# A conv-mixer block on one core: one SBUF operand for VectorE in the projection stage, seven convolution tiles on TensorE, and a new order for loads and first products

## The chip, the cores and the metric

The kernel runs on one core of a Trainium2 chip. The metric is device time in microseconds, the median of several runs on the chip; lower is better. Engines are named as the profile does: PE is TensorE, DVE is VectorE, ACT is ScalarE, POOL is GpSimd, SP is SyncE, whose queue issues almost all transfers here.

## The reference: what is computed

One layer of a decoder block on 256 tokens of width 2048, in float32, with random weights:

```
mod = silu(c) @ mod_w + mod_b                 # 2048 -> 6 x 2048: sh1, sc1, g1, sh2, sc2, g2
h = rms_norm(x, norm1_g) * (1 + sc1) + sh1
u = h @ w_in + b_in                           # 2048 -> 4096
a, gt = split(u);  u = a * sigmoid(gt)
u = depthwise causal convolution of 31 taps over the tokens (u) + dw_b
u = silu(layer_norm(u, ln_g, ln_b))
x = x + (1 + g1) * (u @ w_out + b_out)
h = rms_norm(x, norm2_g) * (1 + sc2) + sh2
x = x + (1 + g2) * (square(relu(h @ mlp_w1)) @ mlp_w2)   # 2048 -> 8192 -> 2048
```

## The kernel before, in words

**Layout.** Channels lie on the 128 partitions, tokens along the free axis: a tile is 128 channels by T=256 tokens, and the width is KT=16 such tiles. Weights come from HBM in float32 in blocks of 1 MB (128 x 16 x 128) into five `raw` buffers. Each block is split into a rounded part `hi` (ACT, L174) and the rest `lo` (DVE or POOL, L175); activations are split in the same way into `hl` tiles (L180, L181). A product is then hi·hi and hi·lo in one 512 wide matmul (L188) and lo·hi in a 256 wide one (L189). There are six half-block buffers for `hi` and six for `lo`.

**Jobs.** `jobs` is 16 input-projection jobs ("in"), 8 output-projection jobs ("out"), then four quarters of 8 "up" and 8 "down" jobs of the MLP. A job makes 256 output channels from all 16 input tiles: 64 matmuls into a PSUM tile `mm`, two of which exist.

**First stage** (L390 to L473). The squares of x (L336) are summed over the channels by PE (L287), and DVE makes the inverse root r (L291 to L307). The first seven in-jobs (HELD = 7) are not run job by job but input tile by input tile: seven PSUM tiles are held open, and for each k `first_mm` (L422) adds the products of the k-th input tile to all of them, in seven steps of six matmuls (L430, L433, L434). Their weights come through three `first` buffers of 0.9 MB. The scale and shift that each k needs come either as columns by DVE (`mod_col`, L259; b = 0 and 3 of the four groups of four k's) or as rows by PE (`mod_chunk`, L197, matmuls at L206, four 1 MB loads per 512 values; b = 1 and 2). In the loop at L438, each row chunk of b = 1 and 2 is followed by two product steps of the group before (L441 to L445).

**In stage** (loop at L634, jobs 7 to 15). Each job's matmuls are followed by the evacuation (`evac`, L383: ACT copies the second half, DVE adds, L387), the gate (L607: sigmoid L609 on ACT, product L613 on DVE) which makes u of this tile, and then by what CONV_AT lists for it. A convolution tile is done in one of two ways. Ten tiles are done by DVE as a chain of taps `acc = u[:, j:j+T] * w[j] + acc` (`conv_steps` L510, `tap` L491): the accumulator is a pair in PSUM, used in turn; the first tap is made by ACT into an SBUF tile `pre` (L502) and enters the third tap as its third operand; in tiles from 4 on the second tap takes the SBUF tile `shift` (L496), which is a common offset (minus the mean of the first two tiles) that is subtracted from every tile and keeps the layer norm's sums small. Six tiles (PE_TILES) are done by PE (`pe_conv` L568): u is written to a DRAM scratch `flat` (L581) and read back as a shifted `wide` tile in four transfers (L584), both on SP's queue, POOL builds diagonal weights (L587), and 64 small matmuls (L598) form the convolution. The last of them, tile 15, copies on chip instead (L570 to L578). Statistics (squares on ACT, sums on PE, L543 to L566) are taken four tiles at a time.

**Layer norm** (L667 to L693). After job 15: mean and mean square (ACT L680, L681; DVE L682, L683), the inverse root on DVE (L298 to L301), then for each pair of tiles the subtraction on POOL (L688), the product on DVE (L689), SiLU on ACT (L692) and the split. x is loaded a second time from POOL's queue (L697) for the residual in the out jobs.

**What sets the order.** All weight and modulation loads stand in one list, `order` (L363 to L375), and are issued on SP's queue in that order as buffers come free (`top_up`, L142); each is bound to be issued after the one before (L153). Everything else is placed by a scheduler that simulates the engines and writes one fixed order per engine; blocks under `urgent()` have priority, and `issue_after` puts an instruction behind a given one. The late modulation chunks (LATE_IN, LATE_OUT) are spread over the jobs and run as rows on PE between them. POOL makes the `lo` halves of all in jobs.

Of the kernel before, what the change touches and what calls it, by code (L numbers as in the profile page):

```python
# [8 lines left out]
F32 = mybir.dt.float32  # L9
# [55 lines left out]
def conv_block(ctx: ExitStack, tc: tile.TileContext, x, vec, dwq, c_row, mod_r, mod_c, w_first, w_in, w_out, w1, w2, out):  # L65
# [18 lines left out]
    xs = []  # L84

    def load_x(pool, queue):
        xs[:] = [pool.tile([P, 4, T], F32, name=f"x{i}") for i in range(4)]
        for i in range(4):
            queue.dma_start(xs[i], x[:, 4 * i : 4 * i + 4, :])

    start_scope = tc.tile_pool(name="start", bufs=1)
    start_pool = start_scope.__enter__()
    load_x(start_pool, nc.sync)
# [7 lines left out]
    modb1 = const.tile([P, KT], F32, name="modb1")  # L101
    nc.vector.tensor_scalar(modb1, col("modb", SC1 * KT, KT), 1.0, None, op0=ALU.add)
# [14 lines left out]
    waiting = {"raw": 0, "first": 0, "cond": 0}  # L117
    room = {"raw": RAW + 1, "first": FIRST + 1, "cond": 1}
    todo = []

    def source(key):
# [13 lines left out]
        if kind == "down":  # L135
            return w2[2 * key[2] + key[3], key[1]]
        return c_row

    def home(key):
        return "first" if key[0] == "first" else "cond" if key == ("c", 0) else "raw"  # L140

    def top_up():  # L142
        while todo and waiting[home(todo[0])] < room[home(todo[0])]:
# [5 lines left out]
            elif tag == "first":  # L149
                raw[key] = start_pool.tile([P, 2 * HELD, P], F32, name="first", bufs=FIRST)  # L150
            else:
                raw[key] = start_pool.tile([P, KT, P], F32, name="cond")
# [83 lines left out]
    def mod_bias(at, n, src):  # L236
        cs = slice(at, at + n)
        nc.vector.tensor_tensor(modc[:, cs], src, col("modb", at, n), op=ALU.add)
        which, k = divmod(at, KT)
        if which in amps:  # L240
            g = col("n1g" if which == SC1 else "n2g", k, n)
            nc.vector.scalar_tensor_tensor(amps[which][:, k : k + n], modc[:, cs], 1.0, g, op0=ALU.add, op1=ALU.mult)
        elif which in (G1, G2):
            nc.vector.tensor_scalar(modc[:, cs], modc[:, cs], 1.0, None, op0=ALU.add)
# [14 lines left out]
    def mod_col(at):  # L259
# [5 lines left out]
        if which == SC1:  # L265
            nc.vector.scalar_tensor_tensor(
                amps[SC1][:, k : k + 1], acc, modb1[:, k : k + 1], col("n1g", k), op0=ALU.add, op1=ALU.mult
# [555 lines left out]
```

## Time and profile before

| what | us |
|---|---|
| three timed runs | 1180.56, 1180.91, 1184.28 |
| median | 1180.91 |
| profiled execution, device time | 1182.57 |
| its span | 1180.8 |
| first product of the first stage | 28.10 |
| start of job 7 (end of the first stage) | 150.69 |
| start of job 8 | 173.67 |
| end of job 15 | about 320.5 |
| first matmul of the out jobs | 358.89 |

The profile is of one execution, recorded by the hardware. A line of a group reads: line of the code, engine, operation, output and inputs by name, shape, number of instructions, then busy time in us and the mean of one in ns, and after the second bar the engine's idle time just before them and what ended it. In the order in time, the two first numbers are the start and the length of a run of like instructions, in us from the start of the span. In the table of stretches, each engine has its busy time and number of instructions; then come the granted clock of TensorE as a share of full speed, the busy share of the 16 transfer engines and their GB/s. TensorE is busy for 95% of the span, but a busy TensorE can be at half clock, and the records of matmuls overlap.

### The profile page before, as it was taken

What the parts mean: (1) busy time and instruction counts of PE and PEld (TensorE: products, weight loads), DVE (VectorE), ACT (ScalarE), POOL (GpSimd) and SP (SyncE); (2) the same over time, 40 slices, a digit from 0 to 9 for tenths busy, and PEclk for the clock granted to TensorE, in tenths of its full rate; (3) what the DMA queues carried; (4) which work ended last, traced back from release to release, by engine and by line L of the source; (5) the groups of instructions that cost most, each with busy time, mean ns of one, the idle gap of its engine ahead of it and who ended that gap; (6) DMA issues with size and microseconds to landing.
All of it is one profiled execution on the core that took longest, in us unless ns stands there. A gap on an engine that the chain in (4) does not pass through costs nothing.

```text
span 1180.8 us, 17239 instructions
## 1 busy us (share of the span) xinstructions
PE 1121.2 (95%) x6962; PEld 936.1 (79%) x6962; DVE 773.3 (65%) x1066; ACT 565.5 (48%) x738; POOL 174.7 (15%) x124
## 2 busy tenths in 40 slices
PE   3959999989968999999999999999999999999998
PEld 2738967656546888888888888888888888888887
DVE  4635889999435797789777555555555556555553
ACT  5234443323336666855444555444555444555441
POOL 0000186545534224300000000000000000000000
PEclk9979999989988999999999999999999999999999
DMA  9998987779977894689888555555555555555640
GB/s 384 419 385 348 408 294 307 282 261 336 300 293 283 304 346 170 253 302 342 290 296 314 178 186 205 180 184 204 183 183 200 189 181 200 189 182 197 209 134 27
DMA packets 46159, 299.04 MB, mean 253 GB/s; under 512 B 5120, under 2 KB 8704, under 8 KB 12800
## 3 DMA queue, kind: packets, MB, share of 16 engines
q1 hardware_dynamic: 45216, 295.17, 68.5%
q0 software_dynamic: 576, 2.10, 0.5%
q8 instruction: 54, 0.88, 0.3%
q10 hardware_dynamic: 288, 0.69, 0.2%
q14 instruction: 25, 0.20, 0.0%
HBM read 295.10 MB, written 2.83 MB: 252 GB/s over the span
## 4 chain that ended last, share of the span: by engine, by line
PE 81%; DVE 14%; DMA 2%; ACT 1%; issue 1%; POOL 0%; SPq 0%; ACTq 0%; POOLq 0%; DVEq 0%
PE mm L188 46%; PE mm L189 24%; DVE acc L498 8%; PE row L206 2%; PE mm L598 2%; DVE raw L264 1%; PE mm L430 1%; PE mm L433 1%; PE mm L434 1%; DMA first<-w_first 1%; PE small L287 1%; DVE acc L496 1%; DVE lo L419 1%; DMA raw<-mod_r 1%; DVE two L387 0%
## 5 line engine op out<-in xcount | busy, mean ns | idle before, releaser
L188 PE MATMUL mm<-hl,hi 128*128 128x512 f32 x1504 | 533.0, 398 | 12.7 <-DVE hl L181 10.3
L174 ACT ACTIVATE hi<-raw 128x1024 fp32r<-128x1024 f32 x324 | 340.5, 1058 | 386.4 <-PE mm L188 356.5
L175 DVE TENSOR_TENSOR lo<-raw,hi 128x1024 fp32r<-128x1024 f32 x272 | 334.0, 1230 | 241.7 <-ACT hi L174 241.0
L189 PE MATMUL mm<-hl,lo 128*128 128x256 f32 x1504 | 424.3, 282 | 0.8 <-POOL lo L175 0.8
L188 PE MATMUL mm<-u,hi 128*128 128x512 f32 x1088 | 377.7, 390 | 0.0
L188 PEld LDWEIGHTS mm<-hl,hi 128*128 128x128 f32 x1504 | 284.1, 189 | 95.1 <-issue 13.0
L189 PE MATMUL mm<-u,lo 128*128 128x256 f32 x1088 | 307.1, 282 | 0.0
L189 PEld LDWEIGHTS mm<-hl,lo 128*128 128x128 f32 x1504 | 286.7, 191 | 8.8 <-issue 6.7
L188 PEld LDWEIGHTS mm<-u,hi 128*128 128x128 f32 x1088 | 204.3, 188 | 43.0 <-DVE small L301 0.2
L189 PEld LDWEIGHTS mm<-u,lo 128*128 128x128 f32 x1088 | 205.6, 189 | 0.0
L175 POOL TENSOR_TENSOR lo<-raw,hi 128x1024 fp32r<-128x1024 f32 x52 | 125.1, 2431 | 74.0 <-ACT hi L174 73.9
L498 DVE SCALAR_TENSOR_TENSOR acc<-u,v,acc 128x256 f32<-128x256 f32 x270 | 107.7, 476 | 0.0
L206 PE MATMUL row<-raw,cz 128*32 128x512 f32 x448 | 63.1, 622 | 12.2 <-DMA raw<-mod_r 11.2
L387 DVE TENSOR_TENSOR two<-mm,two 128x512 f32<-128x512 f32 (+1 forms) x74 | 50.0, 676 | 29.3 <-ACT two L386 28.1
L264 DVE SCALAR_TENSOR_TENSOR raw<-raw 128x2048 f32<-128x2048 f32 x24 | 57.8, 2410 | 13.6 <-DMA raw<-mod_c 10.7
L419 DVE TENSOR_TENSOR lo<-first,hi 128x896 fp32r<-128x896 f32 x32 | 34.3, 1086 | 41.5 <-ACT hi L418 41.5
L386 ACT ACTIVATE two<-mm 128x512 f32<-128x512 f32 (+1 forms) x74 | 42.7, 577 | 38.1 <-PE mm L189 37.6
L418 ACT ACTIVATE hi<-first 128x896 fp32r<-128x896 f32 x32 | 29.6, 944 | 38.0 <-PE mm L433 16.2
L181 DVE TENSOR_TENSOR u<-two,u 128x512 fp32r<-128x512 f32 x40 | 31.2, 779 | 23.4 <-ACT u L180 23.4
L430 PE MATMUL mm<-hl,hi 128*128 128x256 f32 x128 | 37.5, 302 | 8.7 <-ACT hl L180 8.7
L264 DVE SCALAR_TENSOR_TENSOR raw<-raw,cond 128x2048 f32<-128x2048 f32 x16 | 36.4, 2283 | 10.4 <-ACT cond L280 10.4
L433 PE MATMUL mm<-hl,hi 128*128 128x256 f32 x128 | 37.9, 298 | 1.7 <-DVE hl L181 1.7
(140 smaller groups left out, 754.8 us busy)
## 6 DMA issues: line engine op xcount, KB each, us to landing
raw<-w SPq DMA_DIRECT2D x128, 1024.0 KB, 4.9
raw<-mod_r SPq DMA_DIRECT2D x56, 1024.0 KB, 8.8
raw<-mod_c SPq DMA_DIRECT2D x40, 1024.0 KB, 7.3
raw<-w_in SPq DMA_DIRECT2D x18, 1024.0 KB, 8.5
raw<-w_out SPq DMA_DIRECT2D x16, 1024.0 KB, 6.3
first<-w_first SPq DMA_DIRECT2D x16, 896.0 KB, 11.0
wide<-flat SPq DMA_DIRECT2D x20, 142.0 KB, 8.2
x<-x SPq DMA_DIRECT2D x4, 512.0 KB, 6.9
```

Of the source, the lines that this page charges most:

```text
L174: nc.scalar.activation(hi, w[:, ks, :], AF.Copy)
L175: engine.tensor_tensor(lo, w[:, ks, :], hi.bitcast(F32), op=ALU.subtract)
L188: nc.tensor.matmul(p[:, c, :], hi[:, k % HALF, :], m, start=(k == 0), stop=(k == KT - 1))
L189: nc.tensor.matmul(p[:, c, T : 2 * T], lo[:, k % HALF, :], m[:, 0:T], start=False, stop=(k == KT - 1), skip_group_check=True,)
L206: state["row_end"] = nc.tensor.matmul(row_ps[0][32 * k : 32 * k + 32, :], cz[:, 4 * kg + k, 3 - b : 35 - b], w[:, 4 * k : 4 * k + 4, :], s ...
L264: nc.vector.scalar_tensor_tensor(w, w, 1.0, cb, op0=ALU.mult, op1=ALU.mult, accum_out=acc)
L386: nc.scalar.activation(t1, p[:, cs, T : 2 * T], AF.Copy)
L387: nc.vector.tensor_tensor(t2, p[:, cs, 0:T], t1, op=ALU.add)
L419: nc.vector.tensor_tensor(lo, w[:, js, :], hi.bitcast(F32), op=ALU.subtract)
L430: nc.tensor.matmul(p, hi[:, j, :], m[:, 0:T], start=(k == 0 and c == 0), stop=False, skip_group_check=True)
L433: nc.tensor.matmul(p, hi[:, j, :], m[:, T : 2 * T], start=False, stop=False, skip_group_check=True)
L498: nc.vector.scalar_tensor_tensor(out, s, w, acc, op0=ALU.mult, op1=ALU.add)
```

## The change

- **VectorE's operands.** `shift` no longer enters the taps of tiles below 12 (LATER): they are made without it and POOL adds it to four tiles at once (`shift(cvs[...], 4)`) ahead of their statistics. The first tap moves from ACT to DVE, with the bias, straight into the PSUM accumulator; the tile `pre` is gone. The evacuation of in jobs writes in place into PSUM, so that the gate reads PSUM. In the roots of the norms the mean square, its products and (in the layer norm) the factor lie in PSUM, and the square of the first guess is made by ACT. The additions of 1 to the modulation are folded into its bias at the start.
- **Tiles.** PE_TILES gets 9 and 12 and gives up 13: seven convolutions on PE, nine on DVE. Statistics of the first tiles move from after jobs 9, 11, 13 to after jobs 10, 13 and 15.
- **Scratch.** The `flat` transfer of PE tiles below 12 is issued after the last load issued so far at that point of the program.
- **First stage.** The squares of x go through two of the three `first` buffers. For b = 2, eight product steps go ahead of the row chunks, and one or two follow each (LEAD); row chunks are placed behind the last step's matmul.
- **x again.** The four x tiles are entries of the load list, right after the weights of out job 0, so they are issued on SP's queue ahead of the layer norm's end instead of on POOL's behind it. The convolution results move to a pool of their own.

In the order that the scheduler writes for the changed kernel, six row chunks (one more of them stands inside job 7) come ahead of the convolutions of tiles 0 and 1, and both ahead of job 8, where before the two convolutions stood among the first four chunks; three chunks and convolution 9 stand ahead of job 12, and convolution 10 ahead of job 13.

```diff
-PE_TILES = (0, 1, 10, 13, 14, 15)
-CONV_AT = {7: (0, 1, 2, 3), 8: (4,), 9: (5, 6), 10: (7,), 11: (8, 9), 12: (11,), 13: (10, 12), 14: (13,), 15: (14,)}
+PE_TILES = (0, 1, 9, 10, 12, 14, 15)
+CONV_AT = {7: (0, 1, 2, 3), 8: (4,), 9: (5, 6), 10: (7,), 11: (8, 9), 12: (11, 10), 13: (13,), 14: (12,), 15: (14,)}
-UNSHIFTED = (2, 3)
-STAT_AT = {9: 0, 11: 1, 13: 2}
+LATER = 12
+STAT_AT = {10: 0, 13: 1}
+LEAD = {1: 0, 2: 8}
...
-    modb1 = const.tile([P, KT], F32, name="modb1")
-    nc.vector.tensor_scalar(modb1, col("modb", SC1 * KT, KT), 1.0, None, op0=ALU.add)
+    for w in (SC1, G1, SC2, G2):
+        nc.vector.tensor_scalar(col("modb", w * KT, KT), col("modb", w * KT, KT), 1.0, None, op0=ALU.add)
...
     def mod_bias(at, n, src):
         cs = slice(at, at + n)
-        nc.vector.tensor_tensor(modc[:, cs], src, col("modb", at, n), op=ALU.add)
         which, k = divmod(at, KT)
         if which in amps:
             g = col("n1g" if which == SC1 else "n2g", k, n)
-            nc.vector.scalar_tensor_tensor(amps[which][:, k : k + n], modc[:, cs], 1.0, g, op0=ALU.add, op1=ALU.mult)
-        elif which in (G1, G2):
-            nc.vector.tensor_scalar(modc[:, cs], modc[:, cs], 1.0, None, op0=ALU.add)
+            nc.vector.tensor_tensor(src, src, col("modb", at, n), op=ALU.add)
+            nc.vector.tensor_tensor(amps[which][:, k : k + n], src, g, op=ALU.mult)
+        else:
+            nc.vector.tensor_tensor(modc[:, cs], src, col("modb", at, n), op=ALU.add)
...
-    def inverse_root(ms, then=None, where=None):
-        r = tmp.tile([P, T], F32, name="r", bufs=1) if where is None else where
-        q = tmp.tile([P, T], F32, name="q", bufs=1)
-        guess = tmp.tile([P, T], F32, name="guess", bufs=1)
+    def inverse_root(ms, r, then=None):
+        w = two()
+        guess, q = w[:, 0, :], w[:, 1, :]
         nc.scalar.activation(guess, ms, AF.Abs_reciprocal_sqrt)
+        nc.scalar.activation(q, guess, AF.Square)
...
-        nc.vector.tensor_tensor(q, guess, guess, op=ALU.mult)
-        nc.vector.tensor_tensor(q, q, ms, op=ALU.mult)
-        nc.vector.tensor_scalar(q, q, -0.5, 1.5, op0=ALU.mult, op1=ALU.add)
-        nc.vector.tensor_tensor(r, guess, q, op=ALU.mult)
+        nc.vector.tensor_tensor(ms, ms, q, op=ALU.mult)
+        nc.vector.tensor_scalar(ms, ms, -0.5, 1.5, op0=ALU.mult, op1=ALU.add)
+        nc.vector.tensor_tensor(r, ms, guess, op=ALU.mult)
...
-    def evac(p, cs=slice(0, 2)):
+    def evac(p, cs=slice(0, 2), out=None):
         t1 = two()[:, cs, :]
-        t2 = two()[:, cs, :]
+        t2 = two()[:, cs, :] if out is None else out
...
+    sq = [start_pool.tile([P, 2 * HELD, P], F32, name="first", bufs=FIRST) for _ in range(2)]
...
-        s = squares(xs[i])
+        s = squares(xs[i], sq[i % 2])
...
-            for key in first[b]:
-                mods([key])
+            for _ in range(LEAD[b]):
+                next(steps, None)
+            for at, key in enumerate(first[b]):
+                with tc.issue_after(state["step_end"].ins):
+                    mods([key])
                 with tc.issue_after(state["row_end"].ins):
-                    for _ in range(2):
+                    for _ in range(1 + at % 2 if LEAD[b] else 2):
                         next(steps, None)
...
+        if job == ("out", 0):
+            order += [("x", i) for i in range(4)]
...
-        if acc is None and (j > 1 or ct in UNSHIFTED):
+        if j == 0:
+            nc.vector.tensor_scalar(out, s, w, col("dwb", ct), op0=ALU.mult, op1=ALU.add)
+        elif acc is None and ct < LATER:
             nc.vector.tensor_scalar(out, s, w, None, op0=ALU.mult)
...
-    def first_tap(out, ct):
-        s, w = tap_of(ct, 0)
-        nc.scalar.activation(out, s, AF.Identity, scale=w, bias=col("dwb", ct))
...
+            after_load = tc.issue_after(state["load"].ins) if ct < LATER else ExitStack()
             flat = scratch.tile([P, PAD + T + 1], F32, name="flat", bufs=4)
-            nc.sync.dma_start(flat, u[ct])
+            with after_load:
+                nc.sync.dma_start(flat, u[ct])
...
-        if ct >= SHIFT:
+        if ct >= LATER:
             nc.tensor.matmul(p, col("ident", 0, P), state["shift"], start=True, stop=False)
...
-                sg = gate(i, evac(p))
+                sg = gate(i, evac(p, out=p[:, :, 0:T]))
             for ct in CONV_AT.get(n, ()):
                 mix(ct)
             if n in STAT_AT:
+                shift(cvs[STAT_AT[n]], 4)
                 stats(STAT_AT[n])
...
+                shift(cvs[2], 4)
+                stats(2)
...
         if kind == "out":
+            if i == 0:
+                xs = [take(("x", n)) for n in range(4)]
```

More of the change, by code (lines that the diff above doesn't have):

```diff
@@ L512, in conv_steps @@
         rest = tmp.tile([P, T], F32, name="rest", bufs=2)
[L513 to L516 removed]
+        for j in range(TAPS):
+            n = j % 2
+            tap(rest if j == TAPS - 1 else acc[:, n, :], None if j < 2 else acc[:, n, :], ct, j)
             yield
[L518 removed]
+        join(cv(ct), acc[:, 1, :], rest)
     on_dve = [ct for ct in range(KT) if ct not in PE_TILES]
@@ L621, in mix @@
         else:
-            pre[ct] = cp.tile([P, T], F32, name="pre", bufs=2)
-            first_tap(pre[ct], ct)
             conv(ct)
```

115 lines of the change are left out of this document (61 added, 54 removed).

## The prediction

> **What bounds the kernel now.** I read the page first, then the busy time by stretch, then the groups of the in-projection stage, then the order in time at three places. All times are of the profiled execution: span 1180.8 us, device time 1182.57 us, so 1.77 us lie around the span; the median of the three timed runs, 1180.91, is 1.66 below it.
>
> ```profile
> span 1180.8 us, 17239 instructions
> PE 1121.2 (95%) x6962; PEld 936.1 (79%) x6962; DVE 773.3 (65%) x1066; ACT 565.5 (48%) x738; POOL 174.7 (15%) x124
> PE 81%; DVE 14%; DMA 2%; ACT 1%; issue 1%; POOL 0%; SPq 0%; ACTq 0%; POOLq 0%; DVEq 0%
> ```
>
> TensorE carries the chain of waits. VectorE has 14% of it, almost all from the stretch that this change rewrites. By stretch (job 7 up to the start of job 8; jobs 8 to 15; the end of job 15 to the first out-projection matmul; before them the end of the first stage):
>
> ```profile
> core 0: us, PE busy (x) PEld busy (x) DVE busy (x) ACT busy (x) POOL busy (x), PEclk, DMA share, GB/s
> 150.70:173.70 23.00, 23.00 (x227) 14.97 (x227) 21.39 (x51) 9.91 (x17) 18.63 (x13) 1.00 0.92 307
> 173.70:320.30 146.60, 139.17 (x873) 94.01 (x870) 132.75 (x290) 47.31 (x61) 83.33 (x46) 0.95 0.83 301
> 320.30:358.90 38.60, 24.81 (x232) 15.28 (x230) 18.17 (x32) 16.32 (x32) 16.51 (x11) 0.86 0.81 297
> ...
> 110.00:150.70 40.70, 40.47 (x337) 40.19 (x336) 33.88 (x45) 19.47 (x28) 7.45 (x22) 1.00 0.93 384
> ```
>
> The reader is to see that in jobs 8 to 15 VectorE is at 132.75 of 146.6 us, that the transfers are at 0.83 of their engines there, and that the end of the first stage is TensorE work without a gap: 337 matmuls in 40.47 us are 0.12 us each. A product step of the first stage (6 matmuls) is then 0.72 us, a whole k (42) 5.04 us.
>
> The unit prices come from the groups of 150.7 to 358.9:
>
> ```profile
> L498 DVE SCALAR_TENSOR_TENSOR acc<-u,v,acc 128x256 f32<-128x256 f32 x270 | 107.7, 476 | 0.0
> L175 POOL TENSOR_TENSOR lo<-raw,hi 128x1024 fp32r<-128x1024 f32 x41 | 98.4, 2428 | 55.2 <-ACT hi L174 55.1
> ...
> L206 PE MATMUL row<-raw,cz 128*32 128x512 f32 x288 | 38.9, 600 | 1.0 <-PE row L253 0.9 <-DMA raw<-mod_r 0.2
> L598 PE MATMUL mm<-wide,diag 128*32 128x256 f32 x384 | 26.2, 401 | 2.7 <-ACT wide L578 2.7
> ...
> L496 DVE SCALAR_TENSOR_TENSOR acc<-u,v,shift 128x256 f32<-128x256 f32 x8 | 14.4, 1828 | 0.0
> L498 DVE SCALAR_TENSOR_TENSOR acc<-u,v,pre 128x256 f32<-128x256 f32 x10 | 11.7, 1201 | 0.0
> ...
> L609 ACT ACTIVATE sg<-two,v 128x256 f32<-128x256 f32 x9 | 4.6, 509 | 31.2 <-DVE two L387 31.2
> ```
>
> Same engine, same shape, same operation: 476 ns with the accumulator in PSUM, 1828 and 1201 ns where the third operand is an SBUF tile (`shift`, `pre`). Back to back a PSUM tap is shorter still:
>
> ```profile
> 196.68 10.27 DVE L498 SCALAR_TENSOR_TENSOR acc<-u,v,acc 128x256 f32<-128x256 f32 x26
> ```
>
> 10.27/26 is 0.395 us. And the sigmoids waited 31.2 us in nine waits for VectorE's L387: that is where VectorE's load reaches the weight splits, which stand behind the sigmoids on ScalarE, and so TensorE.
>
> **The change part by part.**
>
> *Taps and tiles (VectorE, jobs 7 to 15).* Removed: 8 slow shift taps, 8 x (1.83 - 0.395) = 11.5 us; 10 slow `pre` taps, 10 x (1.20 - 0.395) = 8.1 us; one tile of 31 operations at 0.395, 12.2 us. Added: a first tap on VectorE for nine tiles, 9 x 0.395 = 3.6 us. Together 28 us less VectorE work in 208. A seventh convolution on TensorE adds one sixth of 384 matmuls; the row at 164.17 below gives 3.64 us for 64.
>
> How much of it TensorE sees: jobs 8 to 15 hold 32 pairs of a hi and a lo matmul each; five pairs take 1.73 us (174.13 to 175.86 in the rows below), so a job takes 11.05 us and eight take 88.4; 24 row chunks at about 1.0 (eight matmuls each, 38.9/36 = 1.08 with the overlap of the records), two convolutions of 3.6, sums of about 2.5: 122 us in 146.6. About 20 of the 24.6 us lost I put on VectorE's queue (waits and the half clock after them), 5 on the rest. In the new order the same stretch holds 21 chunks and three convolutions, also 122 us. Without anything new it would take 127 us: **-19.6**.
>
> *Scratch transfers behind the loads (start of job 8).* Of before I quote the sync queue and TensorE, with the landing times of the three row loads (min/median/max):
>
> ```profile
> 150.69 0.50 PE L188 MATMUL mm<-hl,hi 128*128 128x512 f32 x1 [0.23 <-DVE u L613]
> ...
> 164.17 3.64 PE L598 MATMUL mm<-wide,diag 128*32 128x256 f32 x64
> ...
> 167.35 2.56 SPq L154 DMA_DIRECT2D raw<-mod_r  x3
> ...
> 173.67 0.50 PE L188 MATMUL mm<-hl,hi 128*128 128x512 f32 x1
> ...
> 174.13 0.40 PE L188 MATMUL mm<-hl,hi 128*128 128x512 f32 x1
> ...
> 175.86 0.39 PE L188 MATMUL mm<-hl,hi 128*128 128x512 f32 x1
> ```
> ```profile
> DMA to landing us min/median/max: 9.9/11.0/12.6
> ```
>
> Before, the `flat` and `wide` transfers of tiles 0 and 1 stand ahead of the loads of job 9 on the sync queue, and job 8 begins 23.0 us after job 7. After, both `flat`s come behind the two w_in loads of job 9, the `wide`s behind three more mod_r loads; and on TensorE six row chunks, among them those three, stand ahead of both convolutions, and both convolutions ahead of job 8. The three loads can be issued only as the rows ahead of them and the split of job 9's first tile give their buffers back. In before they landed from 167.35 + 9.9 = 177.2 to 182.2, 26.5 to 31.5 us after job 7 began. With the `wide`s after them I take 31 for the last `wide`, then 3.6 + 3.6: job 8 begins 38 us after job 7, **+15**. Low end: if the loads land 5 us sooner because no `wide` is ahead of them, +10. High end: 3 to 4 us more for `wide`s queued behind full loads, +19. What is queued behind it: job 8, the sums of `shift`, and all later splits. The same order is repeated ahead of job 12 (rows of three late loads, then convolution 9): by the same landing times 7 to 9 us, **+9**; it is at nothing if the loads are prefetched during job 11, and at 14 if convolution 10 ahead of job 13 does it again.
>
> *After each new idle time.* The granted clock is seen to halve: 0.50 for the first six us of products, 1.00 after.
>
> ```profile
> 28.00:34.00 6.00, 5.26 (x23) 4.97 (x24) 6.00 (x10) 2.17 (x4) 0.00 (x0) 0.50 1.01 421
> 34.00:40.00 6.00, 6.00 (x50) 5.80 (x50) 5.96 (x9) 1.78 (x4) 0.00 (x0) 1.00 1.00 417
> ```
>
> Six us at half clock lose 3 us; with two new stalls up to 6, and since rows and convolutions dribble in between I take **+4**. (The Trainium skill, "TensorE: Matmul & The Clock Gate", section "What's actually happening", states that an idle window of about 3.4 us halves the clock and about 3.4 us of steady work restores it; by its figure the two dips would be about 3.4 us together, an estimate from that page, and the trace's 6 us stretch is longer. This rule speaks against the change, whose rows leave TensorE idle twice more.)
>
> *Layer norm and the tail.* From the last statistics to the first out-projection matmul:
>
> ```profile
> 344.07 0.42 DVE L682 TENSOR_SCALAR ms<-mm 128x256 f32<-128x256 f32 x1 [18.30 <-ACT mu L681]
> ...
> 345.31 2.56 DVE L242 SCALAR_TENSOR_TENSOR amp<-modc,v 128x4 f32<-128x4 f32 x4
> ...
> 347.79 1.51 DVE L298 TENSOR_TENSOR q<-guess 128x256 f32<-128x256 f32 x1
> ...
> 351.78 4.88 POOL L175 TENSOR_TENSOR lo<-raw,hi 128x1024 fp32r<-128x1024 f32 x2
> 352.00 2.45 DVE L301 TENSOR_TENSOR small<-guess,q 128x256 f32<-128x256 f32 x1
> ...
> 358.89 0.80 PE L188 MATMUL mm<-hl,hi 128*128 128x512 f32 x1 [10.26 <-DVE hl L181]
> ```
> ```profile
> 24.95 0.42 DVE L301 TENSOR_TENSOR r<-guess,q 128x256 f32<-128x256 f32 x1
> ```
>
> The four steps L298 to L301 last from 347.79 to 354.45, 6.7 us, while GpSimd works; the last of them, undisturbed in the first stage, is 0.42. With PSUM operands I take 0.42 for three of them and 0.4 for the square on ScalarE: -5; L242's 2.56 leave the path: -2.5. The convolution of tile 14 and its sums no longer wait for a VectorE chain that ended late: another -2. The tail goes from 38.6 to about 29, **-9.6**; it is at least the 17 us of its TensorE work plus 8 of latency (-13.6), and at worst unchanged but for L242 (-2.5). The reload of x (2 MB) moves from GpSimd's queue to the sync queue, behind the weights of out job 0; the layer norm hides it and I take nothing, with its whole length as the other end: 2 MB at the 421 GB/s of 28 to 34 us above, 5 us.
>
> *At nothing:* the evacuation in place (L387 keeps its shape and length); statistics one job later (their matmuls are the same); the folded `modb` additions at the start; three adds of `shift` on GpSimd in place of one, two more of 128x1024 at about the 2.43 us of L175, hidden by GpSimd's idle 63 of 146.6 us. Without that cover they would hold a split, 5 us.
>
> *The first stage.* The squares of x use the three `first` buffers, and the `first` weights hold them first. In the order of the new kernel x0's square waits for the `lo` of k=0, x1's for that of k=1, and x3's comes behind the `hi` of k=2.
>
> ```profile
> 17.00 1.06 ACT L338 ACTIVATE sq<-x 128x1024 f32<-128x1024 f32 x1 [0.33 <-ACT cond L280]
> ...
> 25.28 1.08 DVE L419 TENSOR_TENSOR lo<-first,hi 128x896 fp32r<-128x896 f32 x1
> ...
> 28.10 0.79 PE L430 MATMUL mm<-hl,hi 128*128 128x256 f32 x2 [8.00 <-ACT hl L180]
> ...
> 33.45 1.08 DVE L419 TENSOR_TENSOR lo<-first,hi 128x896 fp32r<-128x896 f32 x1
> ```
> ```profile
> 32.35 22.82 SPq L154 DMA_DIRECT2D raw<-mod_r  x8
> ```
> ```profile
> 51.10 1.07 PE L206 MATMUL row<-raw,cz 128*32 128x512 f32 x8
> ```
> ```profile
> 75.94 1.94 PE L206 MATMUL row<-raw,cz 128*32 128x512 f32 x8 [9.61 <-DMA raw<-mod_r]
> 77.81 0.58 PE L430 MATMUL mm<-hl,hi 128*128 128x256 f32 x1
> ```
>
> x0's square can start at 26.4 (25.28 + 1.08), x1's near 34.5 (33.45 + 1.08); with that square (1.06) and the two `hi` halves of k=2 (about as long each) x3's starts near 37.5. In before, the last square started at 17.00 and the first product at 28.10, 11.1 us later; so products begin near 48.5 instead of 28.1. Three k's at 5.04 stand ahead of the first row, so that row runs near 65 instead of at or before 51.10; five mod_r loads find buffers, and the sixth, and all behind it on the sync queue, wait for that row. In before all eight had been issued by 55.2 (32.35 + 22.82); now the transfers pause for some 10 us. What is given back: before, the products of k=4 waited 9.61 us for a row load; now eight steps go ahead of those rows. I get the products of k=4 near 84.5 instead of 77.81. From there to job 7 is nearly solid TensorE work (12 x 5.04 + 8 rows at 1.07 = 69 of the 72.9 us from 77.81 to 150.69), so most of the delay stays: **+5.5** (between +1 if the later rows lose their gaps, and +10 if `first` loads stall too).
>
> *Out-projection and MLP:* steadier `hl` tiles, **-1**; nothing else changes there that TensorE's near full stretch would show.
>
> Sum: 5.5 + 15 - 19.6 + 9 + 4 - 9.6 - 1 = **+3.3 us**, on 1182.57: 1185.9. From the median it would be 1184.2. I say 1186. The 0.3% I count from the median 1180.91: 1177.4 and 1184.5 are its ends, so the sum stands just beyond the upper one.
>
> **The rivals.**
>
> *A. The relief reaches TensorE, and the rows are not late (faster).* Mechanism: job 8's start moves by +10 only, the three rows ahead of job 12 are already there, and the first stage loses 1 to 3. Then 2 + 10 - 19.6 + 0 + 2 - 10 - 1 = -16.6, 1166. For it: the load engines were not full in jobs 8 to 15 (0.83). Against it: the sync queue is in order, and the rows' buffers are freed by rows. It decides at job 8's start plus 135 us for the end of job 15: sooner is this case.
>
> *B. Balance.* The same terms with one of the two later losses (9 or 4) at half its price and the first stage at +3: -1.2 to -3.7, 1179 to 1181, within 0.3% (3.5 us, about what a measurement of this kernel can tell from no change).
>
> *C. More stalls (slower still).* The order "late loads, rows, convolution, job" bites a third time ahead of job 13 (+7), and the first stage loses 10: 1182.6 + 3.3 + 7 + 4.5 = 1197. For it: the wide transfers of tile 10 also follow row loads. Against it: after two stalls the loads have run ahead.
>
> *D. The taps do not become shorter,* because the excess is not from the third operand's memory. Of the 28 us taken off VectorE 19.6 are such excess, 0.7; the same share of TensorE's -19.6, 13.7, does not come: 1199.6. Against it stand 270 taps at 476 beside 18 at 1.2 and 1.8 us.
>
> **How the numbers follow.** Forecast (1184.5 to 1192): 0.34. A, 1158 to 1177: 0.27. B: 0.23. C: 0.12. D: 0.04. Faster 0.27; same 0.23; slower 0.34 + 0.12 + 0.04 = 0.50. The range leaves out the faster half of A's low end (below 1165, about 0.10) and the upper end of C with D (above 1199, about 0.08): 1165 to 1199. The forecast's own range is 1184 to 1192; more than half of the chance lies elsewhere, because the sum is a small difference of terms of 10 to 20 us.
>
> **What would show it.** In the changed profile: L496 gone but for one tile, taps all near 0.4 to 0.48; first products near 48 and job 7 near 156; job 8 some 38 us after job 7, TensorE idle ahead of it for row loads; another idle time ahead of job 12 and a half clock behind both; jobs 8 to 15 near 140 us, the tail near 29; out jobs from about 363. The forecast is wrong if job 8 begins within 30 us of job 7, if job 15 ends within 130 us of job 8's start, or if the first stage ends by 152.

## The result, and the profile after

The changed kernel takes 1212.47 us (median of four runs, 1209.48 to 1212.75) beside 1180.74 for the kernel before: a ratio of 1.0263, 95% interval 1.0228 to 1.0298. The forecast was 1186, in a range of 1165 to 1199: slower was right, the size was not. The profiled execution took 1212.75, 30.2 us more than that of before.

The page of the changed kernel: span, engines, and the chain of waits.

```profile
span 1211.0 us, 17330 instructions
PE 1129.6 (93%) x7024; PEld 936.8 (77%) x7024; DVE 741.9 (61%) x1024; ACT 562.5 (46%) x732; POOL 175.3 (14%) x123
PE 69%; DMA 1%; DVE 0%; ACT 0%; issue 0%; DVEq 0%
```

VectorE held 14% of the chain before. This chain does not show that it left: its shares add up to 70%, and its first piece in time begins at 350 us, when the projection stage is almost over.

```profile
350.03 7.67 DMA raw<-mod_r
```

The chains of e5 and e6 below do reach back to the start; VectorE has 2% and 4% of them. VectorE's busy time fell by 31 us, and its taps take 482 ns in the mean, with the offset gone from all tiles but one:

```profile
L513 DVE SCALAR_TENSOR_TENSOR acc<-u,v,acc 128x256 f32<-128x256 f32 x252 | 105.9, 482 | 2.0
```

TensorE's busy time is 8 us higher. Where the 30 us lie is read from milestones. Both kernels, in us from the span's start (in brackets the length of the stretch that ends there):

| milestone | before | after | difference of the stretch | forecast |
|---|---|---|---|---|
| first product | 28.1 | 47.3 | | 48.5 |
| first row chunk | 47.2 | 64.5 | | 65 |
| products of k=4 | 77.8 | 84.9 | | 84.5 |
| start of job 7 | 150.7 | 167.0 | +16.3 | +5.5 |
| start of job 8 | 173.7 (23.0) | 210.6 (43.6) | +20.6 | +15 |
| job 15's evacuation | 320.8 (147.1) | 352.2 (141.6) | -5.5 | -6.6 |
| first out-projection matmul | 358.9 (38.1) | 384.8 (32.6) | -5.5 | -9.6 |
| first wide matmul of the MLP | 458.5 (99.6) | 481.3 (96.5) | -3.1 | -1 |
| last wide matmul of the MLP | 1175.1 (716.6) | 1205.0 (723.7) | +7.1 | 0 |

The first three milestones came within 1.2 us of the forecast; then the first stage lost 10.8 us more than forecast. The sync queue and TensorE of the changed kernel there:

```profile
39.77 31.47 SPq L154 DMA_DIRECT2D raw<-mod_r  x8
```
```profile
47.28 0.79 PE L436 MATMUL mm<-hl,hi 128*128 128x256 f32 x2 [6.28 <-ACT hl L180]
...
64.55 1.06 PE L206 MATMUL row<-raw,cz 128*32 128x512 f32 x8
...
84.88 0.79 PE L436 MATMUL mm<-hl,hi 128*128 128x256 f32 x2 [4.95 <-ACT hl L180]
...
122.18 0.80 PE L436 MATMUL mm<-hl,hi 128*128 128x256 f32 x2 [4.47 <-ACT hl L180]
```

The eight row loads took from 39.77 to 71.24 to be issued, where before they took 22.82 us. What that does to the transfers is seen in the last but one column of the busy time by stretch. First the changed kernel, then the kernel before:

```profile
30.00:60.00 30.00, 20.62 (x113) 18.96 (x114) 20.39 (x29) 11.86 (x18) 0.00 (x0) 0.77 0.77 316
60.00:90.00 30.00, 24.28 (x177) 16.86 (x176) 8.93 (x13) 8.86 (x13) 0.00 (x0) 0.89 0.72 280
90.00:120.00 30.00, 27.71 (x218) 19.84 (x216) 6.46 (x10) 7.52 (x10) 0.00 (x0) 1.00 0.80 332
120.00:150.00 30.00, 27.26 (x198) 26.96 (x199) 27.46 (x34) 13.01 (x19) 0.00 (x0) 0.83 1.01 425
```
```profile
30.00:60.00 30.00, 28.72 (x211) 22.69 (x211) 19.51 (x27) 6.43 (x10) 0.00 (x0) 0.93 1.01 420
60.00:90.00 30.00, 18.12 (x116) 10.01 (x112) 10.70 (x15) 10.77 (x15) 0.00 (x0) 0.72 0.94 385
90.00:120.00 30.00, 29.34 (x240) 26.11 (x237) 17.45 (x24) 12.78 (x17) 0.00 (x0) 1.00 0.85 349
```

From 30 to 120 us the transfers were busy for 2.80 x 30 = 84.0 us before and for 2.29 x 30 = 68.7 us after: 15.3 us of transfer time lost. From 120 to 150 they run at 1.01 and 425 GB/s, where the kernel before was at 0.93 from 110 on, so little is made up, and job 7 comes 16.3 us late. The delay is not all there at k=4, where it is 7.1 us. The second eight row loads are issued 14.5 us later than before (first after, then before):

```profile
82.95 16.02 SPq L154 DMA_DIRECT2D raw<-mod_r  x8
```
```profile
68.47 16.79 SPq L154 DMA_DIRECT2D raw<-mod_r  x8
```

TensorE then waits 4.47 us for the ninth input tile, k=8 (the row at 122.18 above) and works at half clock behind it:

```profile
120.00:130.00 10.00, 7.26 (x32) 6.96 (x33) 9.62 (x12) 4.20 (x7) 0.00 (x0) 0.50 1.02 425
```

The start of job 8, TensorE and the sync queue:

```profile
192.12 1.94 PE L206 MATMUL row<-raw,cz 128*32 128x512 f32 x8 [9.48 <-DMA raw<-mod_r]
194.57 1.94 PE L206 MATMUL row<-raw,cz 128*32 128x512 f32 x8 [0.53 <-DMA raw<-mod_r]
198.63 1.93 PE L206 MATMUL row<-raw,cz 128*32 128x512 f32 x8 [2.12 <-DMA raw<-mod_r]
201.22 9.13 PE L609 MATMUL mm<-wide,diag 128*32 128x256 f32 x128 [0.66 <-DVE acc L513]
```
```profile
177.25 3.86 SPq L154 DMA_DIRECT2D raw<-w_in  x2
181.16 1.08 SPq L592 DMA_DIRECT2D flat<-u  x2
182.33 2.63 SPq L154 DMA_DIRECT2D raw<-mod_r  x3
189.71 9.20 SPq L595 DMA_DIRECT2D wide<-flat  x8
```

This is the forecast mechanism: three late rows, then both convolutions, then job 8. After 9.48 us of idle time the rows take 1.94 us instead of 1.06, at half the clock (granted 0.50 from 192 to 203 us), and the two convolutions 9.13 us instead of 7.3. They begin 34.2 us after job 7. The same picture stands ahead of job 12:

```profile
276.09 1.94 PE L206 MATMUL row<-raw,cz 128*32 128x512 f32 x8 [5.41 <-DMA raw<-mod_r]
...
284.20 5.15 PE L609 MATMUL mm<-wide,diag 128*32 128x256 f32 x64 [1.70 <-DMA wide<-flat]
```

The layer norm's root did become short, 0.43 us a step where it took 1.2 to 2.5:

```profile
379.07 0.43 DVE L298 TENSOR_TENSOR small<-small,two 128x256 f32<-128x256 f32 x1 [0.90 <-ACT two L295]
379.54 0.43 DVE L299 TENSOR_SCALAR small<-small 128x256 f32<-128x256 f32 x1
380.00 0.43 DVE L300 TENSOR_TENSOR small<-small,two 128x256 f32<-128x256 f32 x1
...
384.79 0.77 PE L188 MATMUL mm<-hl,hi 128*128 128x512 f32 x1 [1.56 <-DVE hl L181]
```

And one group in the MLP, which the change does not touch, is slower: the wide matmuls on `u2` (the 32 down jobs and the first two up jobs; the profile leaves the 2 out), 397 ns where the kernel before has 390. First after, then before:

```profile
L188 PE MATMUL mm<-u,hi 128*128 128x512 f32 x1088 | 384.7, 397 | 0.0
```
```profile
L188 PE MATMUL mm<-u,hi 128*128 128x512 f32 x1088 | 377.7, 390 | 0.0
```

1088 times 6.4 ns is the 7.0 us between the two busy times.

### The profile page after: what moved, and what is told of

Read it like the earlier page. It is cut to its first block, busy times and chain, and to the rows that moved or that the text cites. A ratio compares the mean times of both kernels' runs of the same rounds, so it can differ in the third digit from the quotient of the medians.

```text
span 1211.0 us, 17330 instructions
## 1 busy us (share of the span) xinstructions
PE 1129.6 (93%) x7024; PEld 936.8 (77%) x7024; DVE 741.9 (61%) x1024; ACT 562.5 (46%) x732; POOL 175.3 (14%) x123
## 4 chain that ended last, share of the span: by engine, by line
PE 69%; DMA 1%; DVE 0%; ACT 0%; issue 0%; DVEq 0%
PE mm L188 44%; PE mm L189 23%; PE mm L609 1%; DMA raw<-mod_r 1%; PE row L206 0%; PE row L221 0%; PE row L253 0%; PE mm L568 0%; PE mm L575 0%; PE mm L574 0%; PE small L287 0%; ACT acc L711 0%; DVE two L708 0%; DVE x L785 0%; DVE two L390 0%; PE row L233 0%
## 5 line engine op out<-in xcount | busy, mean ns | idle before, releaser
L188 PE MATMUL mm<-u,hi 128*128 128x512 f32 x1088 | 384.7, 397 | 0.0
L188 PEld LDWEIGHTS mm<-hl,hi 128*128 128x128 f32 x1504 | 282.3, 188 | 73.7 <-issue 5.4
L206 PE MATMUL row<-raw,cz 128*32 128x512 f32 x448 | 61.9, 645 | 24.9 <-DMA raw<-mod_r 24.3
L389 ACT ACTIVATE two<-mm 128x512 f32<-128x512 f32 (+1 forms) x74 | 42.5, 575 | 44.1 <-PE mm L189 43.6
L425 DVE TENSOR_TENSOR lo<-first,hi 128x896 fp32r<-128x896 f32 x32 | 34.1, 1088 | 33.9 <-PE acc L439 21.0
L206 PEld LDWEIGHTS row<-raw,cz 128*32 128x32 f32 x448 | 11.7, 112 | 54.5 <-DMA raw<-mod_r 36.7
L436 PE MATMUL mm<-hl,hi 128*128 128x256 f32 x128 | 39.2, 312 | 15.7 <-ACT hl L180 15.7
L390 DVE TENSOR_TENSOR two<-mm,two 128x512 f32<-128x512 f32 (+1 forms) x65 | 43.9, 675 | 14.8 <-ACT two L389 13.6
L436 PEld LDWEIGHTS mm<-hl,hi 128*128 128x128 f32 x128 | 26.7, 212 | 22.1 <-ACT hl L180 16.3
```

The lines of the kernel that those rows point to most:

```text
L188: nc.tensor.matmul(p[:, c, :], hi[:, k % HALF, :], m, start=(k == 0), stop=(k == KT - 1))
L206: state["row_end"] = nc.tensor.matmul(row_ps[0][32 * k : 32 * k + 32, :], cz[:, 4 * kg + k, 3 - b : 35 - b], w[:, 4 * k : 4 * k + 4, :], s ...
L389: nc.scalar.activation(t1, p[:, cs, T : 2 * T], AF.Copy)
L390: nc.vector.tensor_tensor(t2, p[:, cs, 0:T], t1, op=ALU.add)
L425: nc.vector.tensor_tensor(lo, w[:, js, :], hi.bitcast(F32), op=ALU.subtract)
L436: nc.tensor.matmul(p, hi[:, j, :], m[:, 0:T], start=(k == 0 and c == 0), stop=False, skip_group_check=True)
```

## The experiments

All start from the changed kernel. Four edits recur (their main lines):

```diff
# A: squares of x in their own tile
...
-        s = squares(xs[i], sq[i % 2])
+        s = squares(xs[i])
# B: scratch writes free to go
...
-            with after_load:
-                nc.sync.dma_start(flat, u[ct])
+            nc.sync.dma_start(flat, u[ct])
# C: first-stage order as before: no lead, two steps after each row chunk,
#    rows not bound to the last step
...
-                with tc.issue_after(state["step_end"].ins):
-                    mods([key])
+                mods([key])
...
# D: padding behind the constants (D1) and behind the MLP's tiles (D2)
+    nc.gpsimd.memset(const.tile([P, 112], F32, name="cpad"), 0.0)
...
+                nc.gpsimd.memset(mp.tile([P, 64], F32, name="pad"), 0.0)
```

| run | edits | median us | ratio to before (95%) | job 7 | job 7 to out | MLP |
|---|---|---|---|---|---|---|
| before | | 1180.7 | | 150.7 | 208.2 | 716.6 |
| after | | 1212.5 | 1.0263 (1.0228 to 1.0298) | 167.0 | 217.8 | 723.7 |
| e1 | A | 1200.8 | 1.0130 (1.0096 to 1.0164) | 153.7 | 220.0 | 725.1 |
| e2 | B | 1179.8 | 0.9972 (0.9955 to 0.9989) | 166.5 | 183.9 | 723.4 |
| e3 | D2 | 1212.7 | 1.0243 (1.0222 to 1.0264) | 167.1 | 217.2 | 723.6 |
| e4 | C | 1210.1 | 1.0231 (1.0208 to 1.0254) | 165.7 | 217.3 | 726.1 |
| e5 | A B | 1162.5 | 0.9842 (0.9817 to 0.9866) | 151.8 | 183.0 | 723.7 |
| e6 | A B C | 1163.5 | 0.9846 (0.9825 to 0.9867) | 150.3 | 183.9 | 723.4 |
| e7 | D1 | 1206.1 | 1.0212 (1.0173 to 1.0251) | 167.2 | 217.6 | 716.6 |
| e8 | D1 D2 | 1205.0 | 1.0193 (1.0174 to 1.0213) | 167.2 | 217.4 | 716.6 |
| e9 | A B C, ten tiles | 1164.1 | 0.9842 (0.9818 to 0.9866) | 149.9 | 184.5 | 720.4 |
| e10 | A B C, offset in taps | 1163.1 | 0.9847 (0.9816 to 0.9877) | 151.1 | 185.1 | 723.8 |
| e11 | A B C, x late | 1164.9 | 0.9865 (0.9832 to 0.9897) | 156.1 | 183.1 | 724.7 |
| e12 | A B D1 D2 | 1156.4 | 0.9793 (0.9762 to 0.9825) | 153.1 | 183.2 | 716.6 |
| e13 | A B C, first tap as before | 1167.1 | 0.9892 (0.9867 to 0.9917) | 152.7 | 187.9 | 723.4 |
| e14 | A B C, all convolutions as before | 1170.6 | 0.9921 (0.9899 to 0.9944) | 152.7 | 194.6 | 720.3 |
| e15 | A B C, norm as before | 1168.1 | 0.9904 (0.9882 to 0.9926) | 152.0 | 186.6 | 723.9 |
| e16 | e14 and evacuation as before | 1171.5 | 0.9931 (0.9908 to 0.9954) | 153.3 | 197.6 | 720.5 |

The three last columns are of the profiled execution: start of job 7, from there to the first out-projection matmul, and first to last wide matmul of the MLP. Each ratio is to executions of the kernel before that were taken beside the run (their medians lie between 1179.6 and 1182.8), so ratios compare better than medians.

**e1 (A).** 

> Changed kernel, but the squares of x go through a tile of their own again, so that they no longer wait for the three buffers of the first weights. Theory (late squares): the first products started 19 us late, the first row chunk with them, the sync queue stood behind that row and the transfers paused; since both TensorE and the transfers are full to the end of the first stage, the pause is not made up and job 7 starts 16 us late. Then here the first product starts near 28, job 7 near 151 to 153 instead of 167.0, and the time falls by 14 to 16 us to 1197 to 1199. Rival (order of rows): it is the new order of products and row chunks of the third group that leaves TensorE idle and at half clock ahead of the ninth input tile; then job 7 still starts after 160 and the time stays above 1206.

Job 7 at 153.7: the squares are 13.3 of the 16.3 us, and the rival falls. (In the eleven runs with A job 7 lies between 149.9 and 156.1, so 13.3 is good to some 3 us.) The time fell by 11.7 us, less than expected: the stretch from job 7 to the out jobs and the MLP are 2.2 and 1.4 us longer than in the changed kernel. The sync queue shows why: the same eight row loads are issued in 23.20 us again.

```profile
34.47 23.20 SPq L154 DMA_DIRECT2D raw<-mod_r  x8
```

**e2 (B).** 

> Changed kernel, but the scratch writes of the convolution tiles may be issued as soon as they are ready, not behind the last load. Theory (scratch behind loads): job 8 then starts 23 to 25 us after job 7 instead of 43.7, and the wait ahead of job 12 shrinks from 8 us to at most 2; 20 to 26 us less up to the out jobs, of which VectorE's convolutions may take some back, so the time falls by 15 to 26 us to 1187 to 1197. Rival (loads set the pace): the stage is bound by the row and weight loads anyway, so that what is won ahead of job 8 comes back as waits for loads later on; then the out jobs start less than 8 us earlier and the time stays above 1204.

More than either expected: 32.6 us, and the kernel is now 0.3% faster than before although its first stage still loses 16. Job 8 starts 23.0 us after job 7; jobs 8 to 15 take 132.7 instead of 141.6, the rest up to the out jobs 28.2 instead of 32.6. The rival, that the loads would take the gain back, falls. The stretches of e2 (job 7, jobs 8 to 15, up to the out jobs):

```profile
166.50:189.40 22.90, 22.90 (x226) 14.92 (x226) 20.63 (x52) 8.26 (x13) 17.37 (x13) 1.00 0.93 313
189.40:322.00 132.60, 132.60 (x937) 91.64 (x934) 106.44 (x262) 45.06 (x56) 90.68 (x49) 1.00 0.94 342
322.00:350.30 28.30, 25.18 (x230) 14.04 (x228) 10.70 (x30) 17.27 (x34) 10.07 (x8) 0.88 0.72 266
```

Up to the end of job 15 TensorE is busy throughout at a clock of 1.00, and in jobs 8 to 15 the transfers reach 0.94 of their engines (0.83 in before): both resources are nearly full.

**e3 (D2).** 

> Changed kernel with 256 bytes per partition of padding behind the activation tiles of the MLP, so that these tiles lie at the addresses that they had in the kernel before (196320 instead of 196576 and so on); nothing else moves. Theory (address): the wide matmuls of the down jobs took 397 ns in the mean instead of 390 because of where their moving operand lies; then they are back at 390 and the time falls by 7 us to 1205 or 1206. Rival (something else in these jobs, weight splits or transfers): the mean stays at 397 and the time within 2 us of 1212.5.

No effect, 397 ns again: not the address of these tiles.

```profile
L188 PE MATMUL mm<-u,hi 128*128 128x512 f32 x1088 | 384.7, 397 | 0.0
```

**e4 (C).** 

> Changed kernel, but with the order of product steps and row chunks of the kernel before in the first stage (two steps after each row chunk, no lead of eight steps, rows not bound to the last step). The squares stay late. Theory (late squares): job 7 still starts after 160, as the first row remains behind the first products, and the time falls by at most 6 us, to 1206 or more. Rival (order of rows): job 7 starts before 156 and the time falls by 10 us or more, to 1202 or less.

Job 7 at 165.7: the order alone is not the cause.

**e5 (A B).** 

> Changed kernel with both undone: the squares of x in a tile of their own, and the scratch writes free to go as soon as they are ready. Theory (two separate costs): job 7 starts near 153.7 as with the squares alone, job 8 some 13 to 15 us later as with the scratch alone, and the two gains add: 1212.5 - 12 - 32.5, about 1168. Rival (one pace for both): the transfers set the pace of both stages, so the loads that are saved in the first are missing in the second; then at most 6 us less than with the scratch alone, 1174 or more.

The gains add, and by 6 us more than the sum. Job 7 starts at 151.8 and job 8 23.0 us later, as in e2 (the theory's "13 to 15" does not fit e2).

**e6 (A B C).** 

> As the run before, and the old order of product steps and row chunks in the first stage as well. Theory (the new order costs the last 3 us of the first stage): job 7 starts at 150.5 to 151.5 as in the kernel before, and the time falls by another 2 to 3 us, to about 1165. Rival (products ahead of rows help once the squares are early, because the products of the fifth input tile no longer wait for a row load): job 7 starts later than with the new order, by 2 us or more, and the time rises.

Neither. Job 7 came at 150.3 and 151.8 with the two orders, but in the eleven runs with A it lies between 149.9 and 156.1 with no pattern by order, and the times agree within their intervals. What the new order costs or brings is less than these runs can tell.

**e8 (D1 D2) and e7 (D1).** 

> Changed kernel with 448 bytes per partition of padding behind the constants and the 256 behind the activation tiles of the MLP: weight halves, projection activations and MLP activations all lie again as in the kernel before modulo 512 bytes (the halves at 66752 instead of 66304, before 66240). The padding behind the MLP's tiles alone changed nothing. Theory (address of the weight halves against the moving operand): the mean of the wide matmuls of the down jobs falls from 397 to 390 ns, and the time by 7 us, to 1205. Rival (not the address): 397 again, 1211 to 1214.

> Changed kernel with the 448 bytes behind the constants alone: the weight halves lie as before modulo 512 bytes, the MLP's activation tiles stay where the change put them (196576). Both paddings together gave 1205.0. Theory (the weight halves' address alone decides): 390 ns in the mean for the wide matmuls of the down jobs and 1205. Rival (the distance between the two operands decides): a mean above 393 ns and 1208 or more.

390 ns in both; of e7:

```profile
L189 PE MATMUL mm<-u,hi 128*128 128x512 f32 x1088 | 377.7, 390 | 0.0
```

The padding behind the constants alone gives the 7 us back. The seventh tile made the constants 128 bytes longer and a dropped tile 64 shorter, which moved the `raw`, `hi`, `lo` and `hl` tiles by 64 bytes. With `hi` at 66240 (before) and 66752 (e7) the mean is 390, at 66304 (after) 397, at 66176 (e9, e14, e16) the MLP takes 720.3 to 720.5, half-way. These tiles move together, so which of them matters is not settled, nor why the up jobs do not show it.

**e9 (ten tiles).**

```diff
-PE_TILES = (0, 1, 9, 10, 12, 14, 15)
-CONV_AT = {7: (0, 1, 2, 3), 8: (4,), 9: (5, 6), 10: (7,), 11: (8, 9), 12: (11, 10), 13: (13,), 14: (12,), 15: (14,)}
+PE_TILES = (0, 1, 10, 13, 14, 15)
+CONV_AT = {7: (0, 1, 2, 3), 8: (4,), 9: (5, 6), 10: (7,), 11: (8, 9), 12: (11,), 13: (10, 12), 14: (13,), 15: (14,)}
```

> Squares, scratch and first-stage order as before, one SBUF operand in the taps, but ten convolution tiles on VectorE and six on TensorE again, at their old places. Against the same kernel with nine tiles. Theory (after the taps became short, VectorE no longer sets the pace): 12 us more on VectorE are hidden and TensorE saves a convolution of 3.6 us, so between 4 us faster and 1 us slower. Rival (VectorE still sets the pace of jobs 8 to 15): 6 to 12 us slower.

VectorE is busy 9.7 us longer from job 7 to the out jobs, and the stretch is 0.7 us longer: a whole tile more or less on VectorE is worth next to nothing by itself.

**e10 (offset in taps).** Only the first four tiles are shifted by GpSimd.

```diff
-LATER = 12
+LATER = 4
...
-                shift(cvs[STAT_AT[n]], 4)
+                if STAT_AT[n] == 0:
+                    shift(cvs[0], 4)
...
-                shift(cvs[2], 4)
```

> Squares, scratch and first-stage order as before (1163.5), but the offset goes back into one tap of each VectorE tile from 4 on, as an SBUF operand, instead of three adds on GpSimd. Seven slow taps at 1.8 us instead of 0.48 put 9 us on VectorE. Theory (VectorE no longer sets the pace since ten tiles cost nothing): within 2 us of 1163.5, though the slow taps show in the profile. Rival (the slow taps hold GpSimd's weight splits up while they last, not only VectorE): 5 us slower or more.

The time is the same, as the theory says, and the stretch 1.2 us longer, though the seven taps are slow in the mean:

```profile
L506 DVE SCALAR_TENSOR_TENSOR acc<-u,v,shift 128x256 f32<-128x256 f32 x7 | 9.1, 1343 | 0.0
```

**e11 (x late).**

```diff
-        if job == ("out", 0):
-            order += [("x", i) for i in range(4)]
...
-                xs = [take(("x", n)) for n in range(4)]
+                xs = [x_pool.tile([P, 4, T], F32, name=f"x{n}") for n in range(4)]
+                for n in range(4):
+                    nc.gpsimd.dma_start(xs[n], x[:, 4 * n : 4 * n + 4, :])
```

> Squares, scratch and first-stage order as before (1163.5), and x loaded again from GpSimd's queue at the first out job instead of in the sync queue ahead of the norm. Theory (a reload is hidden either way): within 2 us of 1163.5. Rival (the four loads in the sync queue hold a row load and the weights of the second out job up, 4.5 us of TensorE's wait ahead of the out jobs in the changed kernel): 3 to 5 us faster. Second rival (the reload was late before): 2 us slower or more.

1.4 us more, inside the intervals, and the stretch is 0.8 us shorter: the reload is hidden either way.

**e13 (first tap), e14 (all convolutions), e15 (norm), e16 (convolutions and evacuation).** Each puts the old lines back; e14 is e13 with the edits of e9 and e10, e16 is e14 with the last line. Of each edit some lines are shown.

```diff
# e13
-        for j in range(TAPS):
+        for j in range(1, TAPS):
...
+            before = pre.pop(ct) if j == 2 else None if j == 1 else acc[:, n, :]
...
+            nc.scalar.activation(pre[ct], s, AF.Identity, scale=w, bias=col("dwb", ct))
# e15: the layer norm outside urgent(), ms, q and guess in SBUF
-                r = inverse_root(ms, factor[:, 0:T], AF.Silu)
...
+            nc.vector.tensor_tensor(q, guess, guess, op=ALU.mult)
+            nc.vector.tensor_tensor(q, q, ms, op=ALU.mult)
# e16
-                sg = gate(i, evac(p, out=p[:, :, 0:T]))
+                sg = gate(i, evac(p))
```

> Squares, scratch and first-stage order as before (1163.5, first out job at 334.2), and the first tap made by ScalarE into an SBUF tile that enters the third tap, as before. Theory (ScalarE's order: its first taps waited 17.7 us for VectorE with the weight halves queued behind them): 5 to 12 us later at the first out job, 1168 to 1175. Rival (nothing in the taps matters any more): within 2 us of 1163.5.

> As the run before, and also ten tiles on VectorE and the offset as an SBUF operand of the taps: all convolutions as in the kernel before, 28 us of VectorE work put back. Theory (the parts are hidden one by one but not together, since VectorE is then full again): the first out job 12 to 20 us later than 334.2, at 346 to 354. Rival (the gain is the norm's and the evacuation's): 2 to 5 us later.

> Squares, scratch and first-stage order as before, and the layer norm with its root in SBUF and without priority, as before. Theory (the norm is worth what the trace of before showed as slow steps beside GpSimd): the last statistics to the first out job 7 to 9 us longer, 1170 to 1172. Rival (the steps were slow only because VectorE's convolutions ran late): at most 3 us, 1163 to 1166.

> All convolutions as before, and the evacuation of the in jobs into SBUF as before; the norm and the reload of x stay as changed. Theory (VectorE full again): the first out job at 349 to 357, 2 to 4 us after the run with the old convolutions alone, since nine evacuations and gates read two SBUF operands beside GpSimd. Rival (evacuation hidden): no later than that run.

From job 7 to the out jobs, against 183.9: the first tap 4.1 us (2.2 of it ahead of job 8, where e14 with the same edit loses nothing), all convolutions 10.7, the norm 2.8 (3.5 from the last statistics on), convolutions and evacuation 13.8. Each theory was right in kind. Counted from job 7, which began 2 to 3 us later here than in e6, it was too high in size for the first tap, the convolutions and the norm; the evacuation, 3.1 us, came as expected. In e14 the loss is in jobs 8 to 15, 142.9 instead of 132.3, and VectorE is back near full there; first e14, then e6:

```profile
175.70:318.60 142.90, 134.81 (x875) 92.73 (x872) 128.12 (x285) 46.62 (x61) 84.74 (x46) 0.98 0.84 312
```
```profile
173.70:306.00 132.30, 132.30 (x936) 91.63 (x934) 104.78 (x258) 45.20 (x56) 90.92 (x49) 1.00 0.94 344
```

So the parts cost less one by one than together. From job 7 to the out jobs the tenth tile and the offset put 9.7 and 5.6 us of busy time on VectorE and cost 0.7 and 1.2 us; the first tap puts 4.8 us on it and cost 4.1, part of it perhaps the spread of single traces; all three put 23.2 us on it and cost 10.7. In the chains of waits VectorE has 4% in e6 and 11% in e14.

**e12 (A B D1 D2), the best version.** 

> Changed kernel with three things undone: squares of x in a tile of their own, scratch writes free to go, and the two paddings that give weights and activations their old addresses modulo 512 bytes. Theory (the three costs are separate): 1162.5 minus 7, 1155 to 1156. Rival (the address effect appears only beside the late scratch): 1160 or more.

1156.36 us: 2.1% faster than the kernel before (ratio 0.9793, interval 0.9762 to 0.9825) and 4.6% faster than the changed one. The three costs add up, as the theory says.

## Why the prediction was wrong, point by point

- **First stage, +5.5: the step that failed most.** Its first three numbers came true. Then the sentence that begins "From there to job 7 is nearly solid TensorE work" and ends "so most of the delay stays" carried the delay on as TensorE's alone. The delay was 7.1 us at the products of k=4 and grew to 16.3, outside the bounds given (+1 to +10). The pause of "some 10 us" cost 15.3 us of transfer time in transfers that were nearly full (0.93 from 110.00 to 150.70 in the prediction's own table); the next row loads came 14.5 us late, and TensorE waited again and ran at half clock. e1 shows that the late squares are 13.3 of it, e4 that the new order of products and rows is not the cause.
- **Scratch behind the loads, +15 + 9 + 4 = 28: right mechanism, 6 short.** Undoing it alone gives 33.9 back over the stage: 20.6 ahead of job 8, 8.8 in jobs 8 to 15, and 4.4 in the tail, where the forecast had nothing. Ahead of job 8 the sum put the last `wide` at 31 us after job 7, although the row loads ahead of it were to land as late as 31.5; the convolutions began at 34.2. It also missed half the clock on the convolutions themselves (9.13 us where it put 3.6 + 3.6). The Trainium skill ("TensorE: Matmul & The Clock Gate", "What's actually happening") states that an idle window of about 3.4 us puts the clock at half. The trace agrees: behind the 9.48 us of idle time the granted clock was 0.50.
- **Taps and tiles, -19.6: right in kind, too high.** VectorE's relief did reach TensorE, but with the scratch order undone jobs 8 to 15 take 132.7, not 127: -14.4, of which the convolutions are 10.5 (e14). About 3 of the 5.7 us are three row chunks that e2 runs in this stretch (24 instead of the forecast's 21) and not ahead of job 8; the rest is what the step "About 20 of the 24.6 us lost I put on VectorE's queue" took too much. Of the 24.3 us from job 7 to the out jobs between before and e6, convolutions, evacuation and norm put back give 10.7 + 3.1 + 2.8 = 16.6. The forecast had the evacuation at nothing. The other 7.7 us (later statistics, folded bias, priorities) were not taken apart.
- **Jobs 8 to 15 as a whole, -6.6: -5.5, by luck.** The gain was some 5 us smaller than forecast and the loss some 4 us smaller, and the two cancelled.
- **MLP, nothing: wrong, +7.1.** "nothing else changes there" overlooked that a change of the constants' size moves the tiles behind them. e7 shows it.
- **Tail, -9.6: -5.5.** From the statistics to the first matmul it fell from 15.5 us to 8.2, close to the 7.5 worked out for the root and L242; the old norm put back (e15) gives 3.5 of these 7.3. Without the scratch order the tail is 28.2, as forecast (e2); that order cost the other 4.4 us.
- **Rivals.** C had the direction, 1197, with its first stage at +10 and a third stall that did not come. A was the kernel that the order hid: without the three costs it is at 1156 (e12). All three signs of being wrong that the prediction named look to the faster side, and none of them came.

By the table above, 10.8 us of the 26.9 us by which the profiled execution missed the sum are the first stage, 7.1 the address, 5.6 the head of job 8, 4.1 the tail and 1.1 jobs 8 to 15; the out jobs take 2.1 back.

## What to carry to other kernels

Where two resources are both nearly full to the end of a stage, as here, a pause in either may not be made up; look at the transfers' busy share by stretch, and not only at TensorE's, before saying how a delay goes on. A buffer borrowed from a load queue, or a transfer bound behind loads, moves everything behind it in that queue: count what waits there, not the instruction that moved. After a change in the size of any early tile, compare the duration of matmuls that the change does not touch.

## What was not expected of the hardware

The mean of 1088 wide matmuls went from 390 to 397 ns when tiles moved by 64 bytes, and back to 390 when they were padded by 448 more (e7, e8). In the changed kernel's down jobs the pairs of a wide and a narrow matmul start 0.345 and 0.361 us apart in turn, where before all are 0.347 apart.

For the slow taps the prediction named only the SBUF operand. The trace of before shows more: of the 18 taps with `shift` or `pre`, the 11 slow ones (0.83 to 2.63 us) all ran beside a GpSimd instruction, and the 7 with none beside them took 0.47 to 0.48 us. In e10 the first two taps shown have POOL's splits beside them, the other two have nothing:

```profile
210.77 4.75 DVE L506 SCALAR_TENSOR_TENSOR acc<-u,v,shift 128x256 f32<-128x256 f32 x2
...
212.75 5.01 POOL L175 TENSOR_TENSOR lo<-raw,hi 128x1024 fp32r<-128x1024 f32 x2
...
241.69 0.88 DVE L506 SCALAR_TENSOR_TENSOR acc<-u,v,shift 128x256 f32<-128x256 f32 x2
```
